# Feed-forward down projection of a two-layer hybrid decoder: three of four groups by seven half-size products instead of eight

## The chip, the cores and the metric

One core of one Trainium2 chip runs the whole step as one program. The metric is the device time of one execution in microseconds (us). Five engines work from queues of their own, each in order: TensorE (PE, with its weight loads as PEld), VectorE (DVE), ScalarE (ACT), GpSimd (POOL) and SyncE (SP); transfers run beside them.

## The reference, cut to what matters

```python
def swiglu(x, w_gate, w_up, w_down):
    return (jax.nn.silu(x @ w_gate) * (x @ w_up)) @ w_down
...
    for i in range(DEPTH):                       # DEPTH = 2
        h = rmsnorm(x, norm_mix[i])
        ...                                      # layer 0: short convolution, layer 1: retention
        x = x + m
        x = x + swiglu(rmsnorm(x, norm_ffn[i]), ffn_w_gate[i], ffn_w_up[i], ffn_w_down[i])
```

D_MODEL is 1024, the inner width of the feed-forward 2816, and all arithmetic is float32. 512 prompt tokens and 32 sample tokens go through together, as 544 columns.

## The kernel before

Activations lie transposed: `x[0]` to `x[7]` are tiles of 128 features by 544 tokens. A float32 product is made of three fast ones: each operand is split into a high part (ACT copies it to the fast type) and a low part (the rest), and high by high, high by low and low by high are added in PSUM. `split` does this with one ACT copy and one DVE subtraction; `mixed` does it with the low part's second half made by ACT (minus the high part) and a transfer that POOL issues and that adds the weights to it from DRAM.

Each feed-forward (`ffn`) first makes the gate and up projections. Inner tile m and inner tile m + 11 are made together, for m = 0 to 10, by two jobs (`Job`): gate, then up. A job multiplies a 2 by 2 arrangement of weight blocks with a 2 by 2 arrangement of operand blocks (the second split is the tokens, 2 x 272) by seven half-size products instead of eight. The products are called 1, 6, 5, 2, 7, 4, 3 in the order in which PE makes them. In a gate or up job each has 12 matmuls (four tiles of 128 features, three matmuls each). Products 1, 6, 7 and 4 add up in one PSUM bank, and on the way ACT takes snapshots of it: u1 after product 1, u2 after 6, u3 after 7. DVE adds these to the results c11, c22, c21 and c12.

`run` overlaps the jobs: while job i is in its middle (6, 5, 2, 7), the weights of job i+1 are prepared (`weights7`: two loads, four DVE additions or subtractions, four splits); then product 1 of job i+1 is made, and then products 4 and 3 of job i. So between product 7 and product 4 of a job, which both go to the bank that u3 copies, PE has only product 1 of the next job. The weight tiles `w1` and `w3` of a job come from a ring of three buffers: `w1` of the next job can be loaded once `w4` has been computed and `w1` been split.

When the up job of tile m is done, `tail` multiplies gate and up and splits the result u (two tiles of 128 x 544) for the down projection. For groups of three m (0 to 2, 3 to 5, 6 to 8, then 9 and 10) the down projection is made by `down`: for each of the eight tiles n of x it loads 6 blocks of weights (`group_weights`), splits them, makes 6 x 3 matmuls on each half of the tokens, 36 in all, and adds the result to `x[n]` (`residual`). The down products of a group come one m later, behind the up jobs of m = 3, 6 and 9.

The order in which each engine's queue stands is set when the program is built, from the order of the code, buffers and estimated durations; nothing reorders it on the chip, apart from PE's weight loads.

Lines of the profile: L181 matmuls of `project` (`down` uses it), L496 matmuls of jobs, L432 to L435 `mixed`, L450 to L453 the weight sums of `weights7`, L196 and L197 `split`, L556 snapshots, L559 sums with snapshots, L617 to L630 gate and up, L282 `residual`.

## Time and profile before

| | |
|---|---|
| time, median of 3 runs | 1459.03 us (1457.93 to 1459.53) |
| profiled execution, its own time | 1459.07 us |
| its span, first to last instruction | 1457.3 us |
| mean granted TensorE clock | 0.998 |
| feed-forward of layer 1, jobs and three `down` groups | about 1080 to 1400 us of the span |
| instructions PE / DVE / ACT / POOL | 10826 / 1556 / 994 / 191 |
| transfers of POOL's queue (q0) | 30.75 MB, 12.7% of 16 engines' span |

The page and its views are read thus: the chain that ended last tells which engine's work the end hangs on, the windows how full each engine is in a stretch, the timeline when single instructions start and what ended the idle time ahead of them. An instruction's duration there reaches into the next one's start by up to about 0.1 us, so what an engine gets through is read from start to start.

### The profile page before, as it was taken

How to read it: one execution, taken by the hardware profiler on the slowest of the kernel's cores; microseconds unless marked ns; L12 is line 12 of the kernel's file. 1: busy time of each engine (PE TensorE's matmuls, PEld its weight loads, DVE VectorE, ACT ScalarE, POOL GpSimd, SP SyncE). 2: the span in 40 equal slices, each digit the busy share in tenths (PEclk: the TensorE clock that was granted, in tenths of full speed). 3: DMA queues.
4: the chain of work that ended last, by engine and by line, in shares of the span. 5: the costliest groups of instructions: out<-in, count | busy, mean ns of one | idle time of the engine just before them, and what ended most of it. 6: DMA issues, size and time to landing. Idle time of an engine off the chain costs nothing.

```text
span 1457.3 us, 26341 instructions
## 1 busy us (share of the span) xinstructions
PE 1442.1 (99%) x10826; PEld 1365.3 (94%) x10826; DVE 985.2 (68%) x1556; ACT 674.7 (46%) x994; POOL 149.6 (10%) x191
## 2 busy tenths in 40 slices
PE   9999999999999999999999999999999999999997
PEld 9999999999999999999787888878899999999997
DVE  5644688847748648667556685666799848749554
ACT  6222466626526436766422313214376626536334
POOL 0100011101101003211000000000111101001002
PEclk9999999999999999999999999999999999999999
DMA  6222246635536434776544373554666635536422
GB/s 222 79 87 88 89 116 140 148 114 128 145 103 142 125 80 125 198 200 188 208 144 174 116 260 134 187 178 160 191 143 153 153 100 132 134 105 152 123 73 77
DMA packets 86041, 204.61 MB, mean 140 GB/s; under 512 B 8832, under 2 KB 26128, under 8 KB 85664
## 3 DMA queue, kind: packets, MB, share of 16 engines
q1 hardware_dynamic: 67744, 165.37, 34.8%
q0 software_dynamic: 15872, 30.75, 12.7%
q10 hardware_dynamic: 2304, 6.79, 1.2%
q8 instruction: 85, 1.39, 0.4%
q14 instruction: 36, 0.29, 0.1%
HBM read 176.14 MB, written 26.75 MB: 139 GB/s over the span
## 4 chain that ended last, share of the span: by engine, by line
PE 88%; DVE 5%; DMA 3%; issue 1%; ACT 1%; POOL 1%; DVEq 0%; SPq 0%; POOLq 0%; ACTq 0%
PE sm L496 35%; PE mm L181 30%; PE sm L181 7%; PE sm L1049 2%; PE sm L1051 2%; PE sm L1050 2%; PE sm L169 2%; PE sm L171 1%; PE sm L170 1%; PE sm L1275 1%; PE mm L496 1%; DMA w<-in_ffgu_dram 1%; DMA wl<-in_rtqk_dram 1%; DVE S L1298 1%; DVE x L282 1%
## 5 line engine op out<-in xcount | busy, mean ns | idle before, releaser
L196 ACT ACTIVATE wh<-w 128x1024 fp32r<-128x1024 f32 (+4 forms) x120 | 109.4, 916 | 273.7 <-PE mm L181 183.1
L496 PE MATMUL sm<-oh,wh 128*128 128x272 f32 x768 | 222.5, 290 | 0.1
L496 PE MATMUL sm<-ol,wh 128*128 128x272 f32 x768 | 221.3, 288 | 0.2 <-DVE ol L197 0.2
L496 PE MATMUL sm<-oh,wl 128*128 128x272 f32 x768 | 220.8, 287 | 0.0
L282 DVE TENSOR_TENSOR x<-x,mm 128x544 f32<-128x544 f32 x91 | 65.4, 719 | 146.4 <-PE mm L181 146.4
L496 PE MATMUL sm<-oh,h 128*128 128x272 f32 x560 | 161.5, 288 | 0.3 <-ACT oh L196 0.2
L496 PE MATMUL sm<-oh,l 128*128 128x272 f32 x560 | 160.9, 288 | 0.0
L496 PE MATMUL sm<-ol,h 128*128 128x272 f32 x560 | 160.9, 287 | 0.0
L181 PE MATMUL mm<-xh,wh 128*128 128x272 f32 x756 | 157.2, 289 | 0.5 <-ACT wh L196 0.4
L181 PE MATMUL mm<-xh,wl 128*128 128x272 f32 x756 | 156.3, 288 | 0.8 <-DMA wl<-in_rtqk_dram 0.8
L181 PE MATMUL mm<-xl,wh 128*128 128x272 f32 x756 | 156.5, 288 | 0.3 <-DVE xl L211 0.3
L432 ACT ACTIVATE wh<-w 128x1024 fp32r<-128x1024 f32 x103 | 109.1, 1060 | 90.8 <-PE sm L496 62.4
L496 PEld LDWEIGHTS sm<-oh,wh 128*128 128x128 f32 x768 | 144.2, 188 | 2.4 <-ACT gate L556 1.1
L496 PEld LDWEIGHTS sm<-oh,wl 128*128 128x128 f32 x768 | 144.9, 189 | 0.0
L496 PEld LDWEIGHTS sm<-ol,wh 128*128 128x128 f32 x768 | 144.3, 188 | 0.4 <-DVE ol L197 0.4
L197 DVE TENSOR_TENSOR wl<-w,wh 128x1024 fp32r<-128x1024 f32 (+4 forms) x120 | 127.1, 1064 | 23.2 <-ACT wh L196 21.8
L435 POOL DMA_DIRECT2D wl<-in_ffgu_dram x87 | 75.6, 869 | 635.2 <-ACT wl L434 253.2
L181 PEld LDWEIGHTS mm<-xh,wh 128*128 128x128 f32 x756 | 118.9, 188 | 4.6 <-ACT wh L196 1.8
L181 PEld LDWEIGHTS mm<-xh,wl 128*128 128x128 f32 x756 | 118.4, 188 | 1.1 <-DMA wl<-in_rtqk_dram 1.0
L181 PEld LDWEIGHTS mm<-xl,wh 128*128 128x128 f32 x756 | 118.3, 188 | 0.5 <-DVE xl L211 0.5
L197 DVE TENSOR_TENSOR l<-w,h 128x1024 fp32r<-128x1024 f32 x104 | 98.8, 954 | 27.0 <-ACT h L196 26.4
L496 PEld LDWEIGHTS sm<-oh,h 128*128 128x128 f32 x560 | 105.4, 188 | 0.9 <-ACT oh L196 0.6
(319 smaller groups left out, 3313.9 us busy)
## 6 DMA issues: line engine op xcount, KB each, us to landing
w<-in_ffgu_dram SPq DMA_DIRECT2D x88, 512.0 KB
wl<-in_ffgu_dram POOLq DMA_DIRECT2D x87, 256.0 KB, 4.7
w<-in_ffdn_dram SPq DMA_DIRECT2D x96, 192.0 KB
S<-in_rets_dram SPq DMA_DIRECT2D x16, 1024.0 KB
out_rets_dram<-S SPq DMA_DIRECT2D x16, 1024.0 KB
w<-in_cvin_dram SPq DMA_DIRECT2D x21, 512.0 KB
w<-in_rtqk_dram SPq DMA_DIRECT2D x16, 512.0 KB
w<-in_rtg_dram SPq DMA_DIRECT2D x16, 512.0 KB
```

Of the source, the lines that this page charges most:

```text
L169: nc.tensor.matmul(out, lh, rh, start=start, stop=False, skip_group_check=True)
L170: nc.tensor.matmul(out, lh, rl, start=False, stop=False, skip_group_check=True)
L181: last_product[0] = nc.tensor.matmul(half(pt, hf)[:, :HT], w[:, c], act[k][:, hf * HT : (hf + 1) * HT], start=(first and k == ks[0] and i ...
L196: h = nc.scalar.activation(dh, src, AF.Copy)
L197: last_low[0] = nc.vector.tensor_sub(dl, src, dh.bitcast(F32))
L282: last_residual[0] = nc.vector.tensor_add(xk, xk, p)
L432: nc.scalar.activation(wh, w, AF.Copy)
L435: nc.gpsimd.dma_start(wl[:, n:], src[:, n:], accum_op=ALU.add)
L496: last = nc.tensor.matmul(out, w[:, c], b, start=(first and k == 0 and i == 0), stop=(k == KP - 1 and i == 2), skip_group_check=True,)
L1049: nc.tensor.matmul(out, xh[kt][:, ts_], wh[:, cw], start=(kt == 0), stop=False)
L1050: nc.tensor.matmul(out, xh[kt][:, ts_], wl[:, cw], start=False, stop=False)
L1051: last = nc.tensor.matmul(out, xl[kt][:, ts_], wh[:, cw], start=False, stop=(kt == KT - 1))
```

## The change

The down projections of the first three groups are made by jobs of seven products too. A job makes two tiles of x (n and n + 1); the four weight blocks are these two tiles by the two halves of the inner width (the m of the group, and the same m + 11); the operand's four blocks are these halves by the two halves of the tokens. A group has four such jobs, in the same chain of jobs as gate and up, behind the up job of m = 3, 6 and 9. Each product has 9 matmuls (three m, three matmuls each). The last group (9 and 10) is left as it was.

`tail` now makes seven split blocks per m in place of four: four sums `t` (DVE, into the gate tile, which is no longer needed), the split of the three plain blocks by ACT and DVE, the high part of the four sums by ACT, their low part by ACT (minus the high part) and a transfer issued by POOL that adds `t` to it. For m = 3, 6 and 9 the tail is put off until the group's jobs are through, since it writes where these read. `xh` and `xl` become slices of one tile, so that the blocks of two m fit there; the third m of a group goes to the `fp` tiles.

```diff
     def mixed(wh, wl, w, src):
-        n = KP * P
+        n = w.shape[1] // 2
...
-        nc.gpsimd.dma_start(wl[:, n:], src[:, n:], accum_op=ALU.add)
+        nc.gpsimd.dma_start(wl[:, n:], src[:, 1, :] if len(src.shape) == 3 else src[:, n:], accum_op=ALU.add)
...
             def tail(m, g, u):
-                hs, ls = hidden(m)
-                for i in range(2):
-                    split(hs[i], ls[i], u[:, i, :])
+                if m >= last[0]:
+                    hs, ls = hidden(m)
+                    for i in range(2):
+                        split(hs[i], ls[i], u[:, i, :])
+                    return
+                b, t = [v.rearrange("p a (b c) -> p (a b) c", b=2) for v in (u, g)]
+                (h1, h2, ht), (l1, l2, lt) = seven(m)
+                nc.vector.tensor_sub(t[:, 0:2, :], b[:, 1::2, :], b[:, 0:2, :])
+                split(h1, l1, b[:, 0:1, :])
+                split(h2, l2, b[:, 2:4, :])
+                nc.vector.tensor_sub(t[:, 2, :], b[:, 3, :], t[:, 0, :])
+                nc.vector.tensor_sub(t[:, 3, :], b[:, 2, :], t[:, 2, :])
+                nc.scalar.activation(ht, t, AF.Copy)
+                nc.scalar.activation(lt, ht.bitcast(F32), AF.Copy, scale=-1.0)
+                nc.gpsimd.dma_start(lt, t, accum_op=ALU.add)
...
+            def group_jobs(ms):
+                c = slice(ms[0] * P, (ms[-1] + 1) * P)
+                src = a["ffdn"][layer].rearrange("(s n) p c -> n p s c", s=2)
+                def job(n):
+                    made = {}
+                    def take(what, p):
+                        if what == "u3":
+                            made[3] = up_.tile([P, HT], F32, tag="snap", name=nm("snap"), bufs=1)
+                            nc.scalar.activation(made[3], p, AF.Copy)
+                            return
+                        if what[0] == "u":
+                            nc.scalar.activation(halves(sqlast)[:, int(what[1]) - 1, :], p, AF.Copy)
+                            return
+                        kt, hf = n + int(what[1]) - 1, int(what[2]) - 1
+                        at = x[kt][:, hf * HT : (hf + 1) * HT]
+                        nc.vector.tensor_add(at, at, p)
+                        if what == "c22":
+                            nc.vector.tensor_add(at, at, made[3])
+                            nc.vector.tensor_add(x[n], x[n], sqlast)
+                    return Job(
+                        [src[n + i][:, :, c] for i in range(2)], lambda k, which: [t[which] for t in turned[k]], sw, take,
+                        lambda: psum()[:, 0, :], ks=ms,
+                    )
+                return [job(n) for n in range(0, KT, 2)]
...
-                        tail(m, g, u)
+                        if m and m % GROUP == 0:
+                            later[m] = lambda: tail(m, g, u)
+                        else:
+                            tail(m, g, u)
...
-            jobs = [job for m in range(HJ) for job in gate_up(m)]
+            for m in range(HJ):
+                jobs += gate_up(m)
+                if m and m % GROUP == 0:
+                    jobs += group_jobs(groups[m // GROUP - 1])
+                    behind[len(jobs) - 1] = m
...
-            def after(i):
-                m = i // 2
-                if i % 2 and m % GROUP == 0 and m:
-                    down(groups[m // GROUP - 1], list(range(KT)))
+            def after(i):
+                if i in behind:
+                    later[behind[i]]()
```

Counted over the built program, PE has 216 matmuls fewer (10648 to 10432), DVE 294 instructions more, ACT 204 more, POOL 66 transfers more, and SP issues 48 loads fewer (the same bytes, two blocks in one).

Two places show how the queues stand. The first is ACT's queue in the gate job that follows an up job with its tail. `wh`, `wl`, `h` are parts of the next job's weights, `g<-sm` the snapshots u2 and u3 of the gate job, `u<-sm` the snapshot u1 of the next job, `xh<-u` (before) the split of u. Before, behind m = 8:

```order
L556 ACTIVATE g_5357<-sm_5344 128x272
L196 ACTIVATE xh_82<-u_5228 128x544
L196 ACTIVATE h_576_5402<-w_572_5392 128x1024
L432 ACTIVATE wh_5410<-w_5390 128x1024
L434 ACTIVATE wl_5411<-wh_5410 128x512
L556 ACTIVATE g_5357<-sm_5344 128x272
L556 ACTIVATE u_5487<-sm_5474 128x272
```

The same place now; `f<-u` and `f<-g` are the tail's high parts of the first block and of the sums t, `f<-f` is the minus of the latter:

```order
L563 ACTIVATE g_5525<-sm_5512 128x272
L198 ACTIVATE f_5554<-u_5396 128x272
L198 ACTIVATE h_646_5578<-w_642_5568 128x1024
L438 ACTIVATE wh_5586<-w_5566 128x1024
L440 ACTIVATE wl_5587<-wh_5586 128x512
L621 ACTIVATE f_5554<-g_5260 128x1088
L563 ACTIVATE g_5525<-sm_5512 128x272
L622 ACTIVATE f_5555<-f_5554 128x1088
L563 ACTIVATE u_5663<-sm_5650 128x272
```

The copy of the four sums (L621) now stands between the next job's weights and the snapshot u3 (the second `g<-sm`); the minus (L622) stands between u3 and u1. So it is for m = 1, 2, 4, 5, 7 and 8 of both layers; for m = 0 the snapshot u3 comes first.

The second place is DVE's queue in the down projection of layer 0's third group. Before, with `f` and `wl` the low parts of the weights:

```order
L282 TENSOR_TENSOR x_74<-x_74,mm_5656 128x544
L197 TENSOR_TENSOR wl_5743<-w_5739,wh_5742 128x768
L282 TENSOR_TENSOR x_75<-x_75,mm_5701 128x544
L197 TENSOR_TENSOR f_5788<-w_5784,f_5787 128x768
L282 TENSOR_TENSOR x_76<-x_76,mm_5746 128x544
```

Now, one job of two tiles of x (x2 and x3, here `x_76` and `x_77`), from its first result to the last; `mm` and `sm` are PSUM, `l` and `wl` low parts of the next weights, `w` sums of the weights after these:

```order
L650 TENSOR_TENSOR x_77<-x_77,mm_5963 128x272
L199 TENSOR_TENSOR l_694_5936<-w_689_5925,h_693_5935 128x768
L650 TENSOR_TENSOR x_76<-x_76,sm_5973 128x272
L439 TENSOR_TENSOR wl_5944<-w_5923,wh_5943 128x384
L653 TENSOR_TENSOR x_76<-x_76,sqlast 128x544
L652 TENSOR_TENSOR x_77<-x_77,snap_5993 128x272
L457 TENSOR_TENSOR w_705_6031<-w_6029 128x384
L458 TENSOR_TENSOR w_705_6031<-w_705_6031,w_6030 128x384
L459 TENSOR_TENSOR w_6029<-w_6030,w_6029 128x384
L650 TENSOR_TENSOR x_77<-x_77,sm_5892 128x272
L439 TENSOR_TENSOR wl_6040<-w_6030,wh_6039 128x384
L650 TENSOR_TENSOR x_76<-x_76,mm_5963 128x272
```

Two instructions per tile of x have become seven (behind these twelve stand the last split, L199, and the fourth weight sum, L460), and each of the four results waits for its own product on PE.

More of the change, by code (lines that the diff above doesn't have):

```diff
@@ L203, in split_adding, with like @@
         last_minus[0] = nc.scalar.activation(dl, dh.bitcast(F32), AF.Copy, scale=-1.0)
-        nc.gpsimd.dma_start(dl, src, accum_op=ALU.add)
+        nc.gpsimd.dma_start(like(dl, src), src, accum_op=ALU.add)
+    def like(t, src):
+        return t.rearrange("p (s c) -> p s c", s=2) if len(src.shape) == 3 else t
     last_x = [None, None]
@@ L487, in prepare @@
         def prepare(self, adding=False):
-            self.w = weights7(*self.srcs, self.sw, adding, self.spare)
+            self.w = weights7(*self.srcs, self.sw, len(self.ks) * P, adding, self.spare)
         def product(self, out, which, first):
             wh, wl = self.w[which]
-            for k in range(KP):
-                c = slice(k * P, (k + 1) * P)
+            for j, k in enumerate(self.ks):
+                c = slice(j * P, (j + 1) * P)
                 bh, bl = self.operand(k, which)
@@ L497, in product @@
                         out, w[:, c], b,
-                        start=(first and k == 0 and i == 0), stop=(k == KP - 1 and i == 2),
+                        start=(first and j == 0 and i == 0), stop=(j == len(self.ks) - 1 and i == 2),
                         skip_group_check=True,
@@ new lines, in ffn @@
+            later = {}
+            def group_jobs(ms):
[22 more added lines that the diff above has]
+                return [job(n) for n in range(0, KT, 2)]
@@ L658, in down @@
                 held = {m % KP for m in ms if m < HJ - 1}
-                g, lead = len(ms), LEAD if ms[-1] == HJ - 1 else 0
+                g = len(ms)
                 older = [k for k in range(2 * g) if k % g < g - 1]
                 ahead = {}
-                for n in order[:lead]:
+                for n in order[:LEAD]:
                     ahead[n] = group_weights(n, ms), psum()
@@ L673, in down @@
                     residual(n, pt)
-                    if ms[-1] == HJ - 1:
-                        if next_gain is not None and n % KP not in held:
-                            split_x(n, next_gain(n))
-                        square_sum(n, tp, "gu", 4, first=order[0], last=made_in[-1])
-                if next_gain is not None and ms[-1] == HJ - 1:
+                    if next_gain is not None and n % KP not in held:
+                        split_x(n, next_gain(n))
+                    square_sum(n, tp, "gu", 4, first=order[0], last=made_in[-1])
+                if next_gain is not None:
                     for n in order:
@@ L681, in down @@
                             split_x(n, next_gain(n))
-            jobs = [job for m in range(HJ) for job in gate_up(m)]
+            groups = [list(range(m, min(m + GROUP, HJ))) for m in range(0, HJ, GROUP)]
+            last = groups[-1]
+            jobs, behind = [], {}
+            for m in range(HJ):
[3 more added lines that the diff above has]
+                    behind[len(jobs) - 1] = m
             jobs[0].prepare(layer == 1)
@@ L704, in ffn @@
             drain(steps)
-            last = groups[-1]
             late = LATE if layer == 1 else 0
```

44 lines of the change are left out of this document (30 added, 14 removed).

## Prediction

> **What bounds the kernel now.** First the page: engine shares and the chain that ended last.
>
> ```profile
> span 1457.3 us, 26341 instructions
> PE 1442.1 (99%) x10826; PEld 1365.3 (94%) x10826; DVE 985.2 (68%) x1556; ACT 674.7 (46%) x994; POOL 149.6 (10%) x191
> PE 88%; DVE 5%; DMA 3%; issue 1%; ACT 1%; POOL 1%; DVEq 0%; SPq 0%; POOLq 0%; ACTq 0%
> ```
>
> PE is never free, and 88% of the chain is its own work. An average over stages may hide a stage with another bound, so next I read the chain of waits of one cycle of layer 1's feed-forward (three m, then one down projection), and the windows of the same cycle (columns: length, then busy time of PE, PEld, DVE, ACT and POOL, granted clock, DMA share, GB/s).
>
> ```profile
> 1089.99 73.30 PE sm L496 x585
> 1163.29 36.21 PE mm L181 x288
> 1199.50 0.62 PE sm L496 x5
> ```
>
> ```profile
> 1120.00:1160.00 40.00, 40.00 (x322) 40.00 (x321) 34.88 (x55) 28.49 (x44) 6.83 (x8) 1.00 0.61 143
> 1091.00:1164.40 73.40, 73.40 (x587) 73.38 (x587) 64.87 (x101) 50.35 (x77) 11.22 (x13) 1.00 0.63 151
> 1164.40:1200.20 35.80, 35.80 (x287) 35.80 (x286) 16.15 (x23) 7.44 (x9) 0.86 (x1) 1.00 0.34 107
> ```
>
> The chain here is PE alone, at full clock: 40 us hold 322 matmuls, 124.2 ns each. The down projection (L181) is the slack stretch for everybody else: DVE 45% busy against 88% in the gate and up jobs. The change takes work from PE, and puts work on DVE and ACT exactly where they had room.
>
> **What it removes.** A group's down projection had 8 x 36 = 288 matmuls; four jobs of 7 x 9 have 252. Three groups, two layers: 6 x 36 = 216 fewer, at 124.2 ns **26.8 us**. The other end: the chain gives the whole group 36.21 us, 252 at 124.2 ns need 31.3, which is 4.9 per group, 29.4 in all. I take 26.8, since the new matmuls have the shape and line of the jobs, and that is their row. The Trainium skill, "TensorE: Matmul & The Clock Gate", section "Wait — 56ns, not 53.3ns?", gives start to start N ÷ 2.4 GHz plus about 2.5 ns for a warm array: 115.8 ns for 272 columns, an estimate from the page, by which the saving would be 25.0 us; the trace has 124.2 ns, and I go by the trace.
>
> **What a group job costs DVE.** Durations overlap the next start, so I count from start to start (columns: start, duration).
>
> ```profile
> 1100.71 0.71 DVE L197 TENSOR_TENSOR xl<-u,xh 128x544 fp32r<-128x544 f32 x1
> 1101.34 0.68 DVE L197 TENSOR_TENSOR l<-w,h 128x512 fp32r<-128x512 f32 x1
> 1101.95 0.71 DVE L630 TENSOR_TENSOR u<-u,g 128x544 f32<-128x544 f32 x1
> ...
> 1115.01 1.22 DVE L197 TENSOR_TENSOR l<-w,h 128x1024 fp32r<-128x1024 f32 x1
> 1116.15 0.43 DVE L559 TENSOR_TENSOR u<-u,sm 128x272 f32<-128x272 f32 x1
> 1116.50 0.68 DVE L433 TENSOR_TENSOR wl<-w,wh 128x512 fp32r<-128x512 f32 x1
> ```
>
> So 272 elements take 0.35 us, 512 0.61, 544 0.63, 1024 1.14; between them, 384 0.47 and 768 0.87. A job's weights: seven of 384 and one of 768, 4.16. Its results: five of 272 and one of 544, 2.38. Together 6.5 us, beside 63 x 0.1242 = 7.8 us of PE: covered, at 84%. One result has somebody behind it: the sum with `sqlast` (u1 and u2) must be done before ACT overwrites that with the next job's u1, behind which ACT's queue stands; PE needs that u1 two products (2.2 us) after it could be taken. I cost all of this at nothing; PE hides it. If a DVE wait takes that cover away, each of the 24 jobs pays what is over.
>
> **The snapshot u3 in a group job.** It must be through while PE makes one product, now 9 matmuls (1.12 us) instead of 12. ACT's rows in a gate job, and the PE starts beside them:
>
> ```profile
> 1103.26 1.05 ACT L196 ACTIVATE h<-w 128x1024 fp32r<-128x1024 f32 x1
> 1104.52 1.06 ACT L432 ACTIVATE wh<-w 128x1024 fp32r<-128x1024 f32 x1 [0.22 <-PE sm L496]
> 1105.62 0.63 ACT L434 ACTIVATE wl<-wh 128x512 fp32r<-128x512 f32 x1
> 1106.15 0.39 ACT L556 ACTIVATE g<-sm 128x272 f32<-128x272 f32 x1
> 1107.65 0.40 ACT L556 ACTIVATE u<-sm 128x272 f32<-128x272 f32 x1 [1.10 <-PE sm L496]
> ...
> 1112.60 1.12 ACT L620 ACTIVATE g<-g 128x1088 f32<-128x1088 f32 x1
> 1113.62 1.04 ACT L196 ACTIVATE h<-w 128x1024 fp32r<-128x1024 f32 x1
> ```
>
> ```profile
> 1102.93 0.29 PE L496 MATMUL sm<-oh,wh 128*128 128x272 f32 x1
> ...
> 1108.96 0.28 PE L496 MATMUL sm<-oh,h 128*128 128x272 f32 x1
> ```
>
> Product 2 starts at 1102.93 and product 3 at 1108.96; four products (2, 7, 1 of the next job, 4) lie between, 1.51 each, so product 4 starts at 1107.45. ACT starts `wh` some 0.1 us after product 2 (1104.44), since the buffer is product 2's, and reaches u3 1.63 us later. From 1024 elements to 512 the step falls from 1.10 to 0.53 us, so 768 and 384 in their place take 0.3 and 0.1 less: u3 starts 1.2 us later and is done after 1.6. Two products of 9 give PE 2.2 us. Some 0.5 us are left: nothing lost, as long as ACT starts on time.
>
> **The new tail.** DVE had two of 544 (1.26 us); it has two of 544 and three of 272 (2.31): 1.05 more per up job, where the window leaves it (73.4 - 64.87) / 3.5 = 2.4 us idle per pair of jobs. ACT's copy of the four sums, 1088 elements (1.02 us start to start, 1112.60 to 1113.62), now stands ahead of u3 in 12 of the 18 tails. u3 then runs from 1107.17 to 1107.57 instead of from 1106.15 to 1106.54; product 4, due at 1107.45, waits for it and for the handover (0.1 us or so, as between product 2 and `wh`): about 0.25 us, 12 x 0.25 = **3.0 us lost**. The copy needs the last sum from DVE. In DVE's queue that stands behind the 1024 low part, and adding the tail's steps to the rows from 1100.71 on puts its end at about 1106.0: just in time, with 0.1 us to spare. **Any lateness of DVE there goes straight to PE.** The other six cost nothing: for m = 0 u3 comes first, and for the four put off (m = 3 and 6) the copy stands a job's length ahead of the next u3.
>
> **Lateness.** DVE runs its queue on loads that land just in time, and each tail adds a transfer.
>
> ```profile
> 1113.95 0.33 SPq L447 DMA_DIRECT2D w<-in_ffgu_dram  x1
> ```
>
> ```profile
> 1118.05 0.68 DVE L451 TENSOR_TENSOR w<-w,w 128x512 f32<-128x512 f32 x1
> ...
> 1120.66 0.69 DVE L433 TENSOR_TENSOR wl<-w,wh 128x512 fp32r<-128x512 f32 x1 [0.52 <-ACT wh L432]
> ...
> 1149.82 0.69 DVE L451 TENSOR_TENSOR w<-w,w 128x512 f32<-128x512 f32 x1 [0.37 <-DMA w<-in_ffgu_dram]
> ```
>
> ```profile
> q0 software_dynamic: 15872, 30.75, 12.7%
> ...
> L435 POOL DMA_DIRECT2D wl<-in_ffgu_dram x87 | 75.6, 869 | 635.2 <-ACT wl L434 253.2
> ```
>
> ```profile
> 1111.00:1112.00 1.00, 1.00 (x11) 1.00 (x10) 0.90 (x2) 0.42 (x1) 0.81 (x1) 1.00 0.13 21
> 1112.00:1113.00 1.00, 1.00 (x11) 1.00 (x10) 1.00 (x2) 0.80 (x2) 0.06 (x1) 1.00 0.23 27
> ```
>
> The load issued at 1113.95 is used at 1118.05; in another job DVE waited 0.37 us for it. POOL's queue moved 30.75 MB in 12.7% of the span (185 us of all engines), 6 us per MB; a tail's 0.56 MB are 3.3 us. By the rows above u3 ends at 1107.6, the minus copy (1.02) at 1108.6, POOL's issue (0.87) at 1109.5; DMA then has 1.6 us free from 1111 to 1113 (shares 0.13 and 0.23); at most 1.7 us fall on the load. DVE's wait for ACT (0.52) and the 0.1 spare swallow part: between 0 and 1.1 us per tail, up to 13 us. I take 0.2, nearer to nothing because the transfer is issued four microseconds ahead of the load: 12 x 0.2 = **2.4 us**.
>
> **The rest** is free: DVE's 24 jobs against 48 removed tiles are counted above; ACT's 204 more, 0.4 to 1.0 us each, are at most 200 us on an engine idle for 780; POOL's 66 more transfers, 0.87 us each, 57 us on one busy for 150; SP has fewer issues; the program up to the first tail and the last group of each layer are unchanged.
>
> **Sum**, against the profiled execution's own time (1459.07 us; the median of the runs, 1459.03, is the same): 1459.1 - 26.8 + 3.0 + 2.4 = **1437.7 us**.
>
> **Rivals.** (1) *No stall*: ACT and DVE run early enough, u3 makes no wait. For it: the 0.25 us rest on a handover read at one place, and PE had no wait at all in this stretch before. Against: the order of the queue is fixed, and 1.02 us are more than the 0.9 that u3 had to spare. 1459.1 less 26.8 to 29.4: 1430 to 1432. (2) *Group jobs starve*: the loop from `w4` over the load (4.1 us) and seven DVE steps (3.05) to the next `w4` takes 7.15 of 7.8 us; with a load of 5.5 us it takes 8.55, and after two jobs the lead is used up: up to 0.7 us x 16 jobs, 11 us on top, 1444 to 1450. For it: these loads have 1.5 KB rows, like the ones of `down`, whose landing no row here times. Against: DMA share in the group falls from what gate jobs have. (3) *DVE late at the tail's last sum, slower than before*: u3 sits behind a copy that waits for DVE, so PE pays DVE's lateness 1:1, 12 times. It eats the gain from (26.8 - 3.0) / 12 = 2.0 us on; at 3 us the time is 1459.1 - 26.8 + 3 + 36 = 1471. Against: DVE has idle time in each pair, so lateness shouldn't pass from one tail to the next. (4) *The matmuls don't go away*: excluded, the built program has 216 fewer.
>
> **Chances.** Forecast (1433 to 1444) 0.54; (1) 0.14; (2), or lateness near its bound, 0.20; (3) 0.08; (2) and (3) together just giving the gain back 0.04. The range takes in (1) and most of (2) and the bound of lateness: 1430 to 1453. A measurement tells about 0.2% (2.9 us) from no change: faster 0.88, same 0.04, slower 0.08.
>
> **What will show it.** Right: 216 matmuls fewer, PE still above 98% busy, in the group jobs' windows 322 per 40 us; about 0.25 us of PE idle ahead of product 4, put down to the snapshot in ACT, 12 times; DVE above 80% in the group jobs. Wrong: PE waiting for `wl` or `h` in group jobs (rival 2); waits of 1 us or more at the 12 tails with ACT's L621 waiting for DVE (rival 3); waits of DVE for `ffdn` loads; a granted clock below 1.

## The result, and the profile after

| | before | changed |
|---|---|---|
| time, median of 4 runs each | 1458.48 us (1457.86 to 1459.53) | 1433.45 us (1431.7 to 1434.45) |
| ratio | | 0.9826, 95% interval 0.9809 to 0.9843 |
| profiled execution: time, span | 1459.07, 1457.3 | 1431.7, 1429.9 |

The change is faster by 25.0 us, 1.7%; 1437.7 was predicted. First the page of the changed kernel: span, engines and chain.

```profile
span 1429.9 us, 26580 instructions
PE 1416.6 (99%) x10610; PEld 1337.8 (94%) x10610; DVE 1087.4 (76%) x1850; ACT 786.5 (55%) x1198; POOL 207.1 (14%) x257
PE 86%; DVE 6%; DMA 3%; ACT 2%; issue 2%; POOL 1%; DVEq 0%; POOLq 0%; ACTq 0%; SPq 0%
...
q0 software_dynamic: 25376, 50.22, 21.1%
```

The 216 matmuls are gone (10826 to 10610), and PE is as full as before. What they were bought with stands beside it: DVE +102 us, ACT +112, and POOL's accumulating transfers 30.75 to 50.22 MB.

Times of whole executions scatter by one or two microseconds, so the part that the change touches is measured by itself. In every kernel a feed-forward's jobs begin, but for a few products, behind one small matmul group of the norm, and their end is marked by four matmuls of the last down projection, which stand ahead of the last gate and up job's last two products (the first kernel's row shows the second pair of the four). These are PE's rows at both places in the first layer, of the kernel before (columns: start, duration).

```profile
217.09 1.42 PE L240 MATMUL mm<-cb,rN 128*128 128x128 f32 x12
218.35 0.37 PE L496 MATMUL sm<-oh,h 128*128 128x272 f32 x1
...
543.69 0.41 PE L181 MATMUL sm<-xl,wh 128*128 128x272 f32 x2
544.09 0.39 PE L496 MATMUL sm<-oh,wh 128*128 128x272 f32 x1
```

And of the changed kernel:

```profile
215.83 1.42 PE L246 MATMUL mm<-cb,rN 128*128 128x128 f32 x12
217.09 0.37 PE L503 MATMUL sm<-oh,h 128*128 128x272 f32 x1
...
530.64 0.66 PE L183 MATMUL sm<-parts,wh 128*128 128x272 f32 x4
531.29 0.39 PE L503 MATMUL sm<-oh,wh 128*128 128x272 f32 x1
```

From one L496 (L503) start to the other: 544.09 - 218.35 = 325.74 us before, 314.20 after; in the second layer 325.99 and 314.50. The two **stretches** together are 651.73 us before and 628.70 after, 23.0 us shorter. All experiments below are compared by this sum. A second run of the unchanged changed kernel gave 628.36, so a difference of about 0.4 us in such a sum tells nothing.

The group jobs run as predicted. The windows of 40 us in each layer, from the first to beyond the fourth group job (columns as in the prediction):

```profile
286.00:326.00 40.00, 40.00 (x322) 40.00 (x321) 37.37 (x75) 28.08 (x49) 8.35 (x10) 1.00 0.72 160
1144.00:1184.00 40.00, 40.00 (x322) 40.00 (x322) 36.96 (x74) 28.05 (x47) 7.78 (x9) 1.00 0.73 162
```

PE makes its 322 matmuls per 40 us without a gap, though DVE is 92 to 93% busy in these windows, where the down projection left it at 45%.

What PE still loses is in the list of PE's waits (total us, times, longest), of which the kernel before has no PE row:

```profile
PEld sm L503 <- ACT g L563: 4.9, 14, 1.0
...
PE sm L503 <- ACT g L563: 2.0, 4, 0.7
```

L563 is the snapshot. The PE row has 4 waits; the row of the weight loads (PEld) and the single rows have all twelve that were forecast (two of its 14 lie outside the stretches). One of the eight ordinary ones, in ACT, weight load and matmul:

```profile
1114.41 1.10 ACT L621 ACTIVATE parts<-g 128x1088 fp32r<-128x1088 f32 x1
1115.41 0.38 ACT L563 ACTIVATE g<-sm 128x272 f32<-128x272 f32 x1
...
1115.84 0.19 PEld L503 LDWEIGHTS sm<-oh,wh 128*128 128x128 f32 x1 [0.19 <-ACT g L563]
...
1115.58 0.28 PE L503 MATMUL sm<-oh,wl 128*128 128x272 f32 x1
1115.84 0.39 PE L503 MATMUL sm<-oh,wh 128*128 128x272 f32 x1
1116.07 0.29 PE L503 MATMUL sm<-ol,wh 128*128 128x272 f32 x1
```

The copy of the four sums (L621) is followed at once by the snapshot, and 0.05 us after its end product 4 begins. Its first two starts lie 0.26 and 0.23 us behind the one before, where 0.1245 is usual: 0.14 + 0.11 = 0.25 us. The matmul's own row shows no idle time, since its predecessor's duration of 0.28 us covers it; the weight load's row does. Whoever reads only the PE row of the list misses these eight.

At the other four (m = 4 and 7 of the first layer, m = 2 and 4 of the second) the gap, counted in the same way, is 0.87, 0.76, 1.02 and 0.47 us. The first of them, in DVE, ACT and PE:

```profile
332.93 0.69 DVE L458 TENSOR_TENSOR w<-w,w 128x512 f32<-128x512 f32 x1 [2.81 <-DMA w<-in_ffgu_dram]
...
350.14 0.43 DVE L620 TENSOR_TENSOR g<-u,g 128x272 f32<-128x272 f32 x1
```

```profile
350.60 1.11 ACT L621 ACTIVATE parts<-g 128x1088 fp32r<-128x1088 f32 x1 [0.43 <-DVE g L620]
351.62 0.38 ACT L563 ACTIVATE g<-sm 128x272 f32<-128x272 f32 x1
...
352.05 0.39 PE L503 MATMUL sm<-oh,wh 128*128 128x272 f32 x1 [0.60 <-ACT g L563]
```

Here the copy waited for DVE's last sum, and 17 us earlier DVE had stood 2.81 us before a late load. In all the twelve places hold 8 x 0.25 + 3.12 = 5.1 us. A thirteenth gap of the short kind, ahead of the start at 1292.26 us, has nothing to do with the snapshot: its weight load waits for an accumulating transfer of gate and up weights.

### The profile page after: what moved, and what is told of

It is laid out like the page before. It is cut to its first block, busy times and chain, and to the rows that moved or that the text cites. A ratio compares the mean times of both kernels' runs of the same rounds, so it can differ in the third digit from the quotient of the medians.

```text
span 1429.9 us, 26580 instructions
## 1 busy us (share of the span) xinstructions
PE 1416.6 (99%) x10610; PEld 1337.8 (94%) x10610; DVE 1087.4 (76%) x1850; ACT 786.5 (55%) x1198; POOL 207.1 (14%) x257
## 3 DMA queue, kind: packets, MB, share of 16 engines
q0 software_dynamic: 25376, 50.22, 21.1%
## 4 chain that ended last, share of the span: by engine, by line
PE 86%; DVE 6%; DMA 3%; ACT 2%; issue 2%; POOL 1%; DVEq 0%; POOLq 0%; ACTq 0%; SPq 0%
PE sm L503 41%; PE mm L183 17%; PE sm L183 7%; PE mm L503 5%; PE sm L1125 2%; PE sm L1127 2%; PE sm L1126 2%; DMA w<-in_ffgu_dram 2%; PE sm L171 2%; PE sm L173 1%; PE sm L172 1%; PE sm L1351 1%; DVE S L1374 1%; DVE wl L199 1%; DMA wl<-in_rtout_dram 1%
## 5 line engine op out<-in xcount | busy, mean ns | idle before, releaser
L503 PE MATMUL sm<-oh,wh 128*128 128x272 f32 x768 | 223.8, 291 | 2.2 <-ACT g L563 2.0
L503 PE MATMUL sm<-ol,wh 128*128 128x272 f32 x768 | 221.2, 288 | 0.1
L503 PE MATMUL sm<-oh,wl 128*128 128x272 f32 x768 | 220.7, 287 | 0.0
L438 ACT ACTIVATE wh<-w 128x1024 fp32r<-128x1024 f32 (+1 forms) x151 | 149.7, 991 | 82.3 <-PE sm L503 67.4
L503 PE MATMUL sm<-oh,h 128*128 128x272 f32 x560 | 161.3, 288 | 0.0
L503 PE MATMUL sm<-ol,h 128*128 128x272 f32 x560 | 160.8, 287 | 0.0
L503 PE MATMUL sm<-oh,l 128*128 128x272 f32 x560 | 160.6, 287 | 0.0
L183 PE MATMUL mm<-parts,wh 128*128 128x272 f32 x936 | 157.2, 290 | 0.0
L503 PEld LDWEIGHTS sm<-oh,wh 128*128 128x128 f32 x768 | 144.4, 188 | 6.8 <-ACT g L563 4.9
L199 DVE TENSOR_TENSOR l<-w,h 128x1024 fp32r<-128x1024 f32 (+3 forms) x152 | 135.2, 892 | 15.4 <-ACT h L198 12.6
L503 PEld LDWEIGHTS sm<-oh,wl 128*128 128x128 f32 x768 | 144.8, 189 | 0.2 <-DMA wl<-in_ffgu_dram 0.2
L503 PEld LDWEIGHTS sm<-ol,wh 128*128 128x128 f32 x768 | 144.3, 188 | 0.4 <-DVE ol L199 0.4
L183 PEld LDWEIGHTS mm<-parts,wh 128*128 128x128 f32 x936 | 132.9, 189 | 4.1 <-DVE sl L199 0.9
L198 ACT ACTIVATE h<-w 128x1024 fp32r<-128x1024 f32 (+3 forms) x152 | 119.5, 787 | 25.3 <-PE mm L503 14.4
L199 DVE TENSOR_TENSOR wl<-w,wh 128x1024 fp32r<-128x1024 f32 (+3 forms) x96 | 104.4, 1092 | 22.2 <-ACT wh L198 20.7
L439 DVE TENSOR_TENSOR wl<-w,wh 128x512 fp32r<-128x512 f32 (+1 forms) x151 | 97.3, 644 | 30.7 <-ACT wh L438 30.4
L503 PE MATMUL sm<-parts,wh 128*128 128x272 f32 x560 | 108.5, 288 | 0.0
L503 PEld LDWEIGHTS sm<-oh,h 128*128 128x128 f32 x560 | 105.5, 188 | 0.2 <-ACT oh L198 0.2
L503 PEld LDWEIGHTS sm<-oh,l 128*128 128x128 f32 x560 | 105.4, 188 | 0.0
L503 PEld LDWEIGHTS sm<-ol,h 128*128 128x128 f32 x560 | 105.4, 188 | 0.0
```

What stands on the lines that cost most here:

```text
L183: last_product[0] = nc.tensor.matmul(half(pt, hf)[:, :HT], w[:, c], act[k][:, hf * HT : (hf + 1) * HT], start=(first and k == ks[0] and i ...
L198: h = nc.scalar.activation(dh, src, AF.Copy)
L199: last_low[0] = nc.vector.tensor_sub(dl, src, dh.bitcast(F32))
L438: nc.scalar.activation(wh, w, AF.Copy)
L439: nc.vector.tensor_sub(wl[:, :n], w[:, :n], wh[:, :n].bitcast(F32))
L503: last = nc.tensor.matmul(out, w[:, c], b, start=(first and j == 0 and i == 0), stop=(j == len(self.ks) - 1 and i == 2), skip_group_check= ...
```

## Experiments

Names and lines in the diffs are those of the changed kernel. In the list of DVE's waits of the changed kernel the loads have these two rows, which the theories speak of:

```profile
DVE w L458 <- DMA w<-in_ffgu_dram: 17.3, 14, 2.8
...
DVE w L457 <- DMA w<-in_ffgu_dram: 4.4, 3, 2.2
```

All results at a glance (the stretches' sum, and what it is above the changed kernel's 628.70):

| kernel | median us | ratio to before, 95% interval | stretches us | difference |
|---|---|---|---|---|
| u3_first | 1429.63 | 0.9798, 0.9784 to 0.9813 | 623.91 | -4.8 |
| early_sums | 1434.17 | 0.9828, 0.9814 to 0.9843 | 628.49 | -0.2 |
| both | 1429.62 | 0.9797, 0.9783 to 0.9812 | 623.92 | -4.8 |
| double_copy | 1433.62 | 0.9827, 0.9808 to 0.9845 | 629.07 | +0.4 |
| double_held | 1436.99 | 0.9844, 0.9829 to 0.9858 | 631.04 | +2.3 |
| double_pinned | 1447.72 | 0.9923, 0.9909 to 0.9937 | 644.04 | +15.3 |
| no_transfer | 1431.89 | 0.9814, 0.9799 to 0.9828 | 626.46 | -2.2 |
| all_by_dve | 1432.94 | 0.9818, 0.9803 to 0.9832 | 627.36 | -1.3 |
| pieces_by_dma | 1462.19 | 1.0023, 1.0014 to 1.0032 | 657.09 | +28.4 |
| one_group | 1449.07 | 0.9929, 0.9912 to 0.9946 | 643.61 | +14.9 |
| u3_pieces | 1428.85 | 0.9795, 0.9782 to 0.9808 | 623.96 | -4.7 |
| after_again | 1433.47 | 0.9821, 0.9808 to 0.9835 | 628.36 | -0.3 |

### The copy behind the snapshot

```diff
-                nc.scalar.activation(ht, t, AF.Copy)
-                nc.scalar.activation(lt, ht.bitcast(F32), AF.Copy, scale=-1.0)
-                nc.gpsimd.dma_start(lt, t, accum_op=ALU.add)
+                waiting.append((ht, lt, t))
...
                 def gate(what, src):
+                    if what == "u3":
+                        put_sums()
```

`put_sums` makes the three calls taken out above, issued behind the snapshot.

> The changed kernel with the copy of the four sums (L621 of the changed kernel), its minus and its accumulating transfer held back until the gate job's snapshot u3 has been issued; nothing else moves. In the trace of the changed kernel the 12 forecast places (product 4 behind an up job's tail) hold 5.1 us of excess between matmul starts: eight of about 0.25 us, and 0.87, 0.76, 1.02 and 0.47. Theory A (the snapshot waits only because the copy stands ahead of it): all 12 waits of product 4 on the snapshot go, the two job stretches of the layers (313.7 and 314.0 us) become shorter by 4 to 5 us together, and the time is 1428 to 1430. Rival B (the loads, late through the tail's transfer, hold everything up): only the eight waits of 0.25 us go, at most 2 us, and the four long ones remain as waits on loads. Rival C (DVE is late and holds whatever stands at that place): the waits come back at the next DVE result that PE needs (c21 or c12 of the same job), and the stretches change by less than 1 us.

The stretches became 4.8 us shorter, and none of the twelve waits is left. The same place as above, in ACT; L603 is now the copy, and it starts behind the snapshot:

```profile
1113.16 0.64 ACT L440 ACTIVATE wl<-wh 128x512 fp32r<-128x512 f32 x1
1113.69 0.39 ACT L563 ACTIVATE g<-sm 128x272 f32<-128x272 f32 x1
1113.98 1.10 ACT L603 ACTIVATE parts<-g 128x1088 fp32r<-128x1088 f32 x1
```

PE's order is the same in both kernels. The edit also puts off the tail's transfer (for m = 3 of the first layer from 325.51 to 331.82 us), and with it DVE's waits for loads at L458 fell from 17.3 to 11.3 us; at m = 4 of the first layer the load is hardly late any more (0.65 us instead of 2.81). So the place that shows the copy by itself is m = 2 of the second layer. There DVE waits for its load no less than before (1.22 us in the changed kernel), and the stall of 1.02 us is gone all the same:

```profile
1127.15 0.69 DVE L458 TENSOR_TENSOR w<-w,w 128x512 f32<-128x512 f32 x1 [1.48 <-DMA w<-in_ffgu_dram]
```

Theory A holds: DVE's lateness reaches PE through the copy that stands ahead of the snapshot. Since PE's rows show no such gap in these stretches any more, 651.73 - 623.91 = 27.8 us is also what the 216 matmuls were worth.

### The put-off tails' sums at once

```diff
                         if m and m % GROUP == 0:
+                            if m < last[0]:
+                                sums(*[v.rearrange("p a (b c) -> p (a b) c", b=2) for v in (u, g)])
                             later[m] = lambda: tail(m, g, u)
```

`sums` holds the three subtractions, which `tail` then leaves out.

> The changed kernel with the sums on DVE of the two put-off tails in each layer (m = 3 and 6) made at once behind the up job, ahead of the group jobs; the splits into high and low stay put off. Theory A' (the long stalls at the tails of m = 4 and 7 come from DVE, which carries the put-off tail's 1.05 us of sums into the same few jobs): the excess at these places (0.87 and 0.76 us in the first layer, 0.47 at m = 4 of the second) falls to the ordinary 0.25, 1.3 us together, and the first group job of each group takes 1 us of DVE work more with no wait of PE. The 1.02 us at m = 2 of the second layer stays, since no put-off tail is near. Rival B (transfers make the loads late): no change of the four long stalls, 0. Rival D (group jobs have no room on DVE): a new wait of PE in the first group job of up to 1 us at each of 4 places, slower by up to 4 us.

0.2 us, which tells nothing. The edit also changed less than was expected of it, because in the changed kernel two of the put-off tail's three sums already stand in the first group job (the row, and 297.22) and the last right behind it (300.14), with no wait of PE:

```profile
293.07 0.72 DVE L616 TENSOR_TENSOR g<-u 128x544 f32<-128x544 f32 x1
```

The edit left the first where it was and moved the other two 3 to 5 us earlier. So theory A' had a premise that wasn't so: these sums are not carried into the later gate and up jobs. Rival D's extra microsecond in the first group job was there in both kernels and cost nothing in either. DVE waited for its late loads as before (2.42 and 2.64 us where the changed kernel has 2.81 and 2.76). The long stalls at m = 4 and 7 of the first layer were shorter in that run, that at m = 4 of the second was the same, that at m = 2 longer, and a fifth came at m = 7 of the second layer.

> The copy of the four sums behind the snapshot u3, and the put-off tails' sums made at once. Theory A: with the copy out of the way the snapshot waits for nothing of the tail, so the second edit adds nothing measurable to the first: job stretches 4 to 5 us shorter than in the changed kernel, as with the first edit alone, within 0.5 us, and a time of 1428 to 1430 us. Theory A with lateness on DVE that also reaches other results: another 0.5 to 1.3 us beside that. Rivals B and C: at most 2 us shorter.

623.92, the same as with the first edit alone, as theory A had it.

### No accumulating transfer in the tail

```diff
-                nc.gpsimd.dma_start(lt, t, accum_op=ALU.add)
```

> The changed kernel without the tail's accumulating transfer: the low parts of the four sums stay minus the high parts, so that part of the computation is left out (18 transfers of 0.56 MB each). In the trace of the changed kernel VectorE waits for late loads of gate and up weights for 21.7 us in all, 2.8 us at a time, about 19 us ahead of the stalls at m = 4 and 7 and 10 us ahead of that at m = 2. Theory B for the four long stalls (the tail's transfers delay the loads, the late loads make VectorE late, and the copy of the sums waits for VectorE): these load waits fall to less than 8 us in all, the long stalls shrink to the ordinary 0.25, 2 us together, and the eight short ones stay; the time about 1431. Rival (the loads are late because their buffer comes free late behind the group jobs): load waits and long stalls as before, within 0.5 us.

2.2 us shorter, and all twelve gaps are now the short kind of 0.25 us. DVE's waits for these loads fell from 21.7 to 8.7 us:

```profile
DVE w L457 <- DMA w<-in_ffgu_dram: 4.4, 3, 2.2
DVE w L458 <- DMA w<-in_ffgu_dram: 4.3, 8, 2.5
```

What the late load collides with can be seen behind the first group jobs. The put-off tail's transfer (POOL, L623) is issued one microsecond ahead of the load (SPq, L454) that DVE then waits for:

```profile
325.51 0.88 POOL L623 DMA_DIRECT2D parts<-g  x1 [4.65 <-DVE parts L199]
```

```profile
326.57 0.33 SPq L454 DMA_DIRECT2D w<-in_ffgu_dram  x1
```

The windows behind it, and the one queue with any packet from 327 to 330 us, which is POOL's:

```profile
326.00:328.00 2.00, 2.00 (x18) 2.00 (x17) 1.51 (x2) 1.64 (x3) 1.29 (x2) 1.00 0.63 122
328.00:330.00 2.00, 2.00 (x18) 2.00 (x17) 2.00 (x5) 1.32 (x3) 0.65 (x1) 1.00 1.18 154
```

```profile
q0 software_dynamic: 116, 0.50, 112.1%
```

So the load moves nothing for these 3 us. Without the tail's transfer the window from 326 to 328 us is nearly empty for DMA (share 0.09), and DVE's wait at the load is 0.28 us, not 2.81:

```profile
326.00:328.00 2.00, 2.00 (x18) 2.00 (x17) 1.28 (x3) 1.75 (x3) 0.87 (x1) 1.00 0.09 19
```

```profile
331.19 0.69 DVE L458 TENSOR_TENSOR w<-w,w 128x512 f32<-128x512 f32 x1 [0.28 <-DMA w<-in_ffgu_dram]
```

Theory B is right for the four long stalls. The twelve short ones, 3.0 us by the rows, are what is left; the stretches' difference to u3_first, 626.46 - 623.91 = 2.55 us, agrees with it as far as such a sum can tell.

### What an instruction ahead of the snapshot costs

Three runs were needed for one price. The first only doubled the copy:

```diff
                 nc.scalar.activation(ht, t, AF.Copy)
+                nc.scalar.activation(ht, t, AF.Copy)
```

> The changed kernel with the copy of the four sums done twice in a row (the second writes the same numbers again), 1.02 us more of ACT ahead of the snapshot in 12 of the 18 tails. Theory A (the snapshot is just in time but for 0.25 us, so that anything ahead of it goes to PE one for one): 12 waits of 1.2 us or more, the job stretches 11 to 13 us longer together, about 1445 us. Rival B (loads or transfers set the 12 waits): ACT has about 1 us to spare there and the stretches grow by less than 3 us. A price above one for one, over 16 us, would say that the late snapshot also makes later work late, and that lateness is passed on from tail to tail.

0.4 us, not 11 to 13. But the order had changed with it: the kernel's scheduler put the snapshot ahead of both copies in four of the twelve tails and between them in four; in the other four it stayed behind both, but PE's queue had been given more matmuls of the next job ahead of product 4. So the run says nothing on the price. Next, the snapshot was held behind the second copy:

```diff
+                with tc.issue_after(hold[0].ins):
                     last_snapshot[0] = nc.scalar.activation(at["3"], src, AF.Copy)
```

> The copy of the four sums done twice, and the snapshot u3 held behind the second copy in the 12 tails m = 1, 2, 4, 5, 7 and 8 of both layers (with the copy only doubled, the order on ScalarE had changed by itself and the snapshot stood ahead of the copies in most tails, so that the price was not measured). Theory A (whatever stands ahead of the snapshot behind its product 7 goes to PE one for one): 12 times 1.0 us more, the two job stretches about 12 us longer together than in the changed kernel, about 1445 us, and PE waits of 1.0 us and more on the snapshot at all 12 places. Rival (ScalarE has time to spare ahead of the snapshot, and the eight waits of 0.25 us come from something else): less than 4 us.

2.3 us, again far too little, and again the order was the reason: up to nine matmuls of the next job, for which nothing is missing, now stood between product 7 and product 4 and gave ACT the time. Then these matmuls were held behind the current job's product 3. With that, PE's order is that of the changed kernel and ACT's differs by the twelve copies alone (on DVE a few sums changed places with their neighbours):

```diff
+                    with tc.issue_after(behind) if behind is not None else ExitStack():
                         last = nc.tensor.matmul(
```

> The copy of the four sums done twice ahead of the snapshot u3 in the 12 tails, as before, but with TensorE's order held to that of the changed kernel: in the earlier run the kernel's own scheduler had answered the longer copy by putting up to nine matmuls of the next job between product 7 and product 4, so that it measured the scheduler's answer and not the price. Now the only difference is one more instruction on ScalarE at 12 places. Theory A (the snapshot has nothing to spare there): one for one, 1.0 to 1.15 us at each of the 12, the two job stretches 12 to 14 us longer together than the 628.7 us of the changed kernel, about 1446 us; at the places that are late already by VectorE no less. Rival (part of the second copy is covered by waiting that is there anyway): 6 us or less.

15.3 us, and PE's list of waits has all twelve places in one row:

```profile
PE sm L507 <- ACT g L574: 15.8, 12, 2.1
```

An ordinary place went from 0.25 us to 1.39 (1.28 at the first start and 0.11 at the next). In ACT the second copy is the whole difference, 1.02 us from its start to the snapshot's and 1.13 from the first copy's start to the second's:

```profile
255.69 1.10 ACT L636 ACTIVATE parts<-g 128x1088 fp32r<-128x1088 f32 x1
256.82 1.11 ACT L638 ACTIVATE parts<-g 128x1088 fp32r<-128x1088 f32 x1
257.84 0.38 ACT L574 ACTIVATE g<-sm 128x272 f32<-128x272 f32 x1
```

```profile
258.27 0.39 PE L507 MATMUL sm<-oh,wh 128*128 128x272 f32 x1 [1.12 <-ACT g L574]
```

One for one, then: 1.14 us more at an ordinary place, and 13.9 us more at the twelve places together, the worst of which has now 2.24 us at its first start. That is the size that theory A expected. The other 1.4 us of the 15.3 are something else. Behind that worst wait the fourteen matmuls from 1149.12 to 1152.43 us start about 0.227 us apart instead of 0.1245, and the granted clock is 0.50 there:

```profile
1149.50:1152.40 2.90, 2.90 (x14) 2.90 (x14) 0.04 (x1) 1.24 (x3) 0.87 (x1) 0.50 0.74 207
```

In double_held a gap of 2.43 us from start to start was followed by full clock, so the length of the wait alone doesn't decide it; what does stays open.

### The low parts of the first pieces

The changed kernel makes one half of each first piece's low part on DVE and the other by a minus on ACT and an accumulating transfer. Two runs move that split to either end, in the group jobs only. In both PE's order stays as it is.

```diff
-        (split_adding if adding else mixed)(*p1, w1, src1)
+        by = split_adding if adding else mixed if n == KP * P else (lambda h, l, w, src: split(h, l, w))
+        by(*p1, w1, src1)
...
-        mixed(*p3, w3, src2)
+        (by if n < KP * P else mixed)(*p3, w3, src2)
```

> In the group jobs both halves of each first piece get their low part by a subtraction on VectorE, with no minus on ScalarE and no accumulating transfer: two subtractions of 384 more in each of the 24 group jobs, about 1.0 us by the 0.69 us of one of 512 and its neighbours' distance, so VectorE goes from 6.5 to 7.5 us of a job's 7.8 (96%). Theory A (VectorE's time in group jobs is spare up to the length of the job): no wait of PE on weights in group jobs, stretches within 1 us of the changed kernel's, the time 1432 to 1435. Rival 2 of the prediction (the loop from one job's last weights to the next job's loads is what limits, and starves PE once VectorE is near full): 0.3 us and more lost in each of 24 jobs, slower by 7 us and more, with waits on wl or h in the group jobs.

The window of the four group jobs of the changed kernel, and of this one:

```profile
286.00:317.00 31.00, 31.00 (x250) 31.00 (x249) 29.08 (x60) 19.92 (x37) 6.99 (x8) 1.00 0.69 156
```

```profile
286.00:317.00 31.00, 31.00 (x250) 31.00 (x249) 30.80 (x58) 17.12 (x29) 0.13 (x1) 1.00 0.39 116
```

DVE goes from 94% to 99% busy, and PE has the same 250 matmuls. The expected "nothing" is confirmed and a little more: the stretches are 1.3 us shorter, the long stalls, now at m = 4 and 7 of both layers, have 0.3 to 0.4 us at the first start of product 4 instead of 0.4 to 0.9. With 9.4 MB less by accumulating transfers (40.78 instead of 50.22) that fits theory B; that it is the cause was not tried apart from DVE's added work.

The other end takes `by = split_adding if adding or n < KP * P else mixed`. There the low part of the first half of the second piece becomes another number, because that half has been overwritten by a difference when the transfer adds the weights from memory; the work is that of the split.

> In the group jobs the first pieces get both halves of their low part by a minus on ScalarE and an accumulating transfer, none by VectorE: 48 transfers grow from 0.19 to 0.38 MB, VectorE has 1.0 us less in each of 24 jobs, ScalarE as much more. Where all of it was done by VectorE the stretches became 1.3 us shorter. Theory B (what the transfers cost is late loads, which make VectorE late at the next gate and up jobs' tails): VectorE's waits for loads of gate and up weights stay at 20 us or rise, and the stretches grow by 0 to 3 us. Rival (VectorE's load in the group jobs is what makes it late): the long stalls at m = 4 and 7 go, 1 to 2 us shorter.

Neither expectation came near: 28.4 us longer, the whole gain and a little more. PE's list of waits, the landing time of the transfers, and the same window:

```profile
PE sm L504 <- DMA wl<-in_ffdn_dram: 22.5, 17, 3.3
```

```profile
wl<-in_ffdn_dram POOLq DMA_DIRECT2D x48, 384.0 KB, 5.5
```

```profile
286.00:317.00 31.00, 27.48 (x215) 26.83 (x214) 22.71 (x45) 19.35 (x31) 8.35 (x7) 1.00 0.84 182
```

The changed kernel's row of these transfers has 4.4 us for 192 KB:

```profile
wl<-in_ffdn_dram POOLq DMA_DIRECT2D x48, 192.0 KB, 4.4
```

PE waits in 17 places for the transfers themselves, the longest 3.3 us, and DVE waits 23.5 us for the loads of the group jobs, which were no more than 1 us late in all when the changed kernel was run again. The four group jobs pass 215 matmuls instead of 250. This is the starvation of the prediction's second rival, by transfers rather than by DVE: in the group jobs the way of the weights through ACT, POOL and the DMA queues has less to spare than the engine that is 94% busy. All of that way has grown: ACT's minus from 0.53 to 0.84 us, POOL's issue from 0.87 to 1.20, the landing from 4.4 to 5.5; the run doesn't tell their parts from each other, nor from the later loads. Behind the longest wait the granted clock fell to 0.50 here too, for 3.4 us.

### One group only

```diff
-                if m and m % GROUP == 0:
+                if m and m % GROUP == 0 and m // GROUP - 1 in by_jobs:
                     jobs += group_jobs(groups[m // GROUP - 1])
...
+                if i in plain:
+                    down(plain[i], list(range(KT)))
```

Here `by_jobs` is `(0,)`, and `down` is the loop of the kernel before.

> Only the first of the three groups of each layer by jobs of seven products; the other two by the loop down with its buffers, as in the kernel before. If the gain lies in the groups' matmuls alone, less a cost for each tail, it is the same for each group: of the 23.1 us by which the two job stretches of the layers became shorter, 7.7 stay, the stretches are 15.4 us longer than in the changed kernel and the time is about 1450. Rival (what the first group gains is paid in the later ones, whose group jobs and put-off tails follow one another): the first group alone gains 10 us or more.

The stretches are 651.73 - 643.61 = 8.1 us shorter than before, where 7.7 is a third of the whole gain: as far as such a sum can tell, the groups do not pay for each other. The median is 9.9 us below before's; by it the rival's 10 could not be excluded, by the stretches it can.

### The best version, and the changed kernel again

> The two edits that shortened the stretches together: the copy of the sums behind the snapshot, and the group jobs' first pieces by VectorE alone. Theory: with the copy out of the way no wait of PE is left in the stretches (624 us together), so the second edit adds nothing there: within 0.5 us of the first alone, 1429 to 1430. Rival (fewer transfers help beside that): 1 us or more shorter than the first alone.

623.96: nothing beside the first edit's 623.91, as expected where no wait is left to remove. Its 1428.85 us are the lowest median of all, 4.6 us below the changed kernel on the same chip.

> The changed kernel once more, on the same chip as the three others: 1432 to 1435, its stretches 628.7 us within 1 us, four long stalls and eight short ones at the same tails. If the long stalls are at other places or of other lengths, they hang on the transfers' timing in that run, and the differences of 1 us between kernels above say little.

The same four long stalls and a fifth small one (m = 7 of the second layer), of 0.6, 0.4, 0.7, 0.4 and 0.4 us at the first start, against 0.76, 0.65, 0.91 and 0.36 in the first run: they come back at the same four places, and how long they are, and whether m = 7 of the second layer is among them, varies from run to run.

## Why the prediction was right, step by step

- **Bound and matmuls removed: right.** 216 fewer, PE 99% busy, 322 per 40 us in the group jobs. 26.8 us were taken and 29.4 was the other end; 27.8 were measured once nothing else stood in the way (u3_first against before), 128.8 ns for each matmul where the row had 124.2. The 115.8 ns estimated from the formula that the Trainium skill gives ("TensorE: Matmul & The Clock Gate", section "Wait — 56ns, not 53.3ns?") would have been 25.0 us; the measurement decides against it here.
- **Group jobs cost DVE nothing: right, and so was its load.** 6.5 of 7.8 us, 84%, was worked out from start to start. In one full turn of the first layer's group jobs, from 301.95 to 309.83 us, DVE's rows are just the fourteen instructions that were counted, 6.5 us of 7.88. The windows of 31 and 40 us show 92 to 94% because they count durations, which overlap (88% in this one job), and because other jobs' results and the put-off sums fall into them. The conclusion held up to 99% (all_by_dve).

```profile
301.95:309.83 7.88, 7.88 (x65) 7.88 (x64) 6.92 (x15) 5.09 (x9) 1.75 (x2) 1.00 0.76 170
```

- **Snapshot in a group job: right**, no wait of PE there.
- **The copy ahead of u3, 12 x 0.25 = 3.0 us: right in mechanism, place and size.** 0.25 us is what the rows show at the eight ordinary places and, without the tail's transfer, at all twelve. That what is late ahead of the snapshot goes straight to PE was shown by double_pinned, one for one, for ACT. DVE's lateness takes the same way through the copy, but most of it is made up before it gets there: 2.81 us of waiting at a load became 0.62 us more at the snapshot, 0.87 instead of 0.25.
- **Lateness, 12 x 0.2 = 2.4 us: right in cause, wrong in place, and in its sum lucky in part.** 2.2 us go with the tail's transfer. But the 0.2 was a choice between 0 and 1.1; the lateness sits at four tails, 0.2 to 0.8 us each, and is nothing at the other eight. Three of the four follow the transfer of a put-off tail, which the prediction had counted as free: "the other six cost nothing" is true of the copy and not of the transfer.
- **Rival 1 (no stall)** is what u3_first makes of the kernel: 1429.6, where 1430 to 1432 was worked out. **Rival 2** was not seen in the changed kernel; it came when the group jobs' transfers were doubled. **Rival 3** exists as a mechanism (copy waiting for DVE), at 0.5 to 1.0 us in four places instead of 2 us in twelve.

The time came out 4.2 us below the forecast. Of that, 0.6 is the profiled execution of before, which stands above the median (1459.07 and 1458.48), and 1.6 are the two terms above (27.8 - 26.8, and 5.4 - 4.8). The other 2.0 us lie outside the stretches, and their cause stays open. The profile of before has 7.2 us from its last output's issue (1450.05) to the end of the span, that of the changed kernel 4.15:

```profile
1450.05 0.33 SPq L765 DMA_DIRECT2D out_yT_dram<-yb  x1
```

```profile
1425.75 0.33 SPq L841 DMA_DIRECT2D out_yT_dram<-yb  x1
```

The instructions there are the same. All profiles of kernels with the change have 4 to 5 us and the only one of before has 7, so whether the program or that one execution makes the difference can't be said.

## What to carry to other kernels

Before counting an engine's work as free, ask what stands behind it in its queue: 1.02 us of copy ahead of a snapshot cost 0.25 us a time with PE 99% busy, and moving it one place back, with its transfer, gave 4.8 us, a fifth of the gain. When a step trades matmuls for preparation, the share of the preparing engine says less than the transfers: with DVE at 99% nothing was lost, with 9.4 MB more by accumulating transfers 28 us. And where a scheduler sets the order, an added cost is not an experiment until the other engines' order is held: the same copy showed 0.4, 2.3 and 15.3 us, and of the last 1.4 us were a slower clock behind one wait.

## What the runs showed of the hardware that was not expected

The accumulating transfers had nearly the same price per MB in three kernels: 12.7% of 1457.3 us of 16 engines for 30.75 MB before, 21.1% for 50.22 MB in the changed kernel and 25.0% for 59.66 MB in pieces_by_dma are each about 6 us of all engines per MB. What grew with their size is the time until they land: 4.4 us for 192 KB, 5.5 for 384 KB over the program, and 6.2 in the window of the first group jobs. Of pieces_by_dma, the queue's row on the page and the transfers of that window:

```profile
q0 software_dynamic: 31520, 59.66, 25.0%
```

```profile
wl<-in_ffdn_dram POOLq DMA_DIRECT2D x7, 384.0 KB, 6.2
```

Two more things are told above with their rows. A load that was issued one microsecond behind POOL's transfer moved no packet for 3 us. And in two runs the granted clock was 0.50 for 3.4 us behind a long wait of PE, of 2.4 us from start to start in double_pinned and 3.6 in pieces_by_dma, while a gap of 2.43 us in double_held was not followed by it.
